# Two block rows of eight products instead of three at the head of the feed-forward input, and another order of the weight sums

## The chip, the cores and the metric

The kernel runs on one core of one Trainium2 chip. The metric is the device time of one execution in microseconds, lower is better. Four compute engines take part: PE (TensorE, the matmuls), DVE (VectorE), ACT (ScalarE) and POOL (GpSimd); SP (SyncE) issues nearly all DMA transfers from one queue, in the order in which they stand there. Each engine works through its own list of instructions in order, and semaphores make one engine wait for another.

## The reference, cut to what matters

One inference step of a two-layer backbone: 512 latent tokens and 128 prompt tokens (T = 640), width 1024, attention in each layer, and behind each attention a gated feed-forward part of inner width 2816. Everything is float32. The part that the change touches is this:

```python
def swiglu(h, w_in, w_out):
    gate, up = jnp.split(h @ w_in, 2, axis=-1)
    return (jax.nn.silu(gate) * up) @ w_out
...
        hp = modulate(rms_norm(xp, norm_ffn[l]), sh2_p, sc2_p)
        hs = modulate(rms_norm(xs, norm_ffn[l]), sh2_s, sc2_s)
        xp = xp + g2_p * swiglu(hp, w_ffn_in[l], w_ffn_out[l])
        xs = xs + g2_s * swiglu(hs, w_ffn_in[l], w_ffn_out[l])
```

## The kernel before, in words

**Layout.** Activations stand feature-major: a tile has 128 features on the partitions and 640 tokens along it, cut in two halves of 320 (HT). The width 1024 is eight such tiles (KT), the inner width 2816 is 22 block rows of 128 (FB).

**Three passes per product.** A float32 operand is split into a high part (a copy in the multiplier's format, made by ACT) and a low part (the rest, by DVE). A product of two operands is then three matmuls: high with high, high with low, low with high (mm3). The first two of the three need only the weight's high part. A matmul of one 128x128 weight tile with one half is 128x320.

**Block row of eight.** For one block row fb, `whole` computes gate and up over both halves: 2 outputs x 2 halves x 8 feature tiles x 3 passes = 96 matmuls. Its two weight tiles (wgu, 128x1024 each, gate and up) are loaded, split by ACT (L173) and DVE (L174), and used as they are. The eight products of the name are gate and up, two halves of tokens, two halves of the width.

**Block row of seven.** All other block rows use a scheme of Strassen's kind on the 2x2 blocks (gate/up by width halves, and token halves by width halves): 7 products of 4 feature tiles x 3 passes = 84 matmuls. It needs sums of the weights and sums of the activations. `seven` makes the weight sums of a row from the two raw tiles ru (up) and rg (gate): wX is ru itself, wW the second half of rg; s13 (L1208, L1209) and s24 (L1212, L1213) are 128x1024 sums built in halves of 512, and wY and wZ are their splits. `split` does the splitting (ACT L1400, DVE L1401). The activation sums D, N, C, E are made once per layer by `add_up` (L316 to L327) from float32 copies of the modulated activations. The seven products go into three PSUM banks, fg, fd and fu, in the order of `ffn`'s second loop: wX with the first block (fg), wY with D (fd), the E product of the row before (`close`), wZ with N (fg), wX with the third block (fu), wZ with the fourth (fd), wY with C (fg). Copies and sums between them (p, u, up, g) are ACT's and DVE's.

**What sets the order.** The code issues work row by row, and the framework's scheduler, at build time, moves each engine's instructions by their dependences and its own costs; so the order on an engine isn't the order of the code. Loads into `rawp` share three buffers of 128x1024, loads into the pool fp under the tag "wr" two buffers in layer 0 and one in layer 1, and a load waits until the last reader of its buffer is done. In layer 0 the two "wr" buffers also hold float32 copies of the activations until `add_up` has read them. The split tiles alternate between two pools (`turn`).

**Around the head of the stage.** Behind attention comes a norm whose two halves end in a matmul with ones (oanp in layer 0, ocnp in layer 1), a logarithm and exponential on ACT (L221, L222), and `ModS.make` (L296 to L314): DVE's multiplication by the norm (h01t or h11t), ACT's or DVE's scale and shift (h32), a high part and a low part (h01q, h11q). In layer 1 the output stage also works with seven products, and `hidden_pair` makes its operands on the fly: for a pair of block rows the tiles op..a, D, N, b, c, C, E, each with an ACT copy, a DVE low part (L1428) and, for most pairs, a store to DRAM (sp..).

Of the kernel before, what the change touches and what calls it, by code (L numbers as in the profile page):

```python
# [11 lines left out]
F32 = mybir.dt.float32  # L12
F32R = mybir.dt.float32r
AF = mybir.ActivationFunctionType
ALU = mybir.AluOpType
# [3 lines left out]
P = 128  # L19
# [32 lines left out]
def body(ctx, tc, xT, vecs, crow, wm0, wm0g1, wm0g, wm1, wA, wNV, wNA, wMK, wMV, wOA, wGQ, wGK, wGV, wOC,  # L52
# [3 lines left out]
    V, S, G = nc.vector, nc.scalar, nc.gpsimd  # L56
# [32 lines left out]
    def bank(name, kind="m"):  # L89
        if kind == "m":  # L90
            return psp.tile([P, 512], F32, tag="m", bufs=4, name=name)
        return ypool["pool"].tile([P, 512], F32, tag=kind, bufs=ypool["tags"][kind], name=name)
# [13 lines left out]
    def f(ap):  # L106
        return ap.bitcast(F32)
# [60 lines left out]
    def unit(src, n, name, lo="v", pool=None, bufs=3):  # L168

        raw = load(src, n, name + "r")  # L170
        t = (pool or wp).tile([P, 2, 1024], F32R, tag="w", bufs=bufs, name=name)
        hi, lw = t[:, 0, :n], t[:, 1, :n]
        S.activation(hi, raw, AF.Copy)  # L173
        (V if lo == "v" else G).tensor_tensor(lw, raw, f(hi), ALU.subtract)  # L174
        return hi, lw
# [350 lines left out]
    with tc.tile_pool(name="start", bufs=1) as big:  # L526
# [14 lines left out]
        m = [mod0(j, lambda j=j: bank(f"mod{j}", "m"), lambda j, half: [raws[j, half][:, q, :] for q in range(2)]) for j in range(4)]  # L541
# [607 lines left out]
                box["m"].make(c, nrm.rs, k)  # L1149
        return box, nxt  # L1150

    FEW = 3, 3
    STAY = 3
    FIRST, SECOND = FO_ORDER[:9], FO_ORDER[9:]

# [42 lines left out]
    def seven(ru, rg, name, fp, split):  # L1198

        n = ru.shape[-1]  # L1200
        m = n // 2
        wX = split(ru, f"wX{name}")
        t = fp.tile([P, 2, 512], F32R, tag="w4", bufs=2, name=f"wW{name}")
        wW = t[:, 0, :m], t[:, 1, :m]
        S.activation(wW[0], rg[:, m:], AF.Copy)
        V.tensor_tensor(wW[1], rg[:, m:], f(wW[0]), ALU.subtract)
        s13 = fp.tile([P, 1024], F32, tag="ws", bufs=2, name=f"s13{name}")[:, :n]
        V.tensor_tensor(s13[:, :m], rg[:, :m], rg[:, m:], ALU.add)  # L1208
        V.tensor_tensor(s13[:, m:], ru[:, :m], rg[:, :m], ALU.add)  # L1209
        wY = split(s13, f"wY{name}")  # L1210
        s24 = fp.tile([P, 1024], F32, tag="ws", bufs=2, name=f"s24{name}")[:, :n]
        V.tensor_tensor(s24[:, :m], s13[:, m:], rg[:, m:], ALU.add)  # L1212
        V.tensor_tensor(s24[:, m:], s24[:, :m], ru[:, m:], ALU.add)  # L1213
        wZ = split(s24, f"wZ{name}")
        return wX, wW, wY, wZ

    def ffn_out_seven(x, nxt, opened, ops, spilt, split, close, last):
# [30 lines left out]
        class Block:  # L1248


            def __init__(self, i, n, c0):
                self.pairs, self.n, self.name = PASSES[i], n, f"o{i}_{n}"
                self.end = i == len(PASSES) - 1
                self.m = m = P * len(self.pairs)
                ru, rg = raw(n, c0, 2 * m, f"ru{self.name}"), raw(n + 4, c0, 2 * m, f"rg{self.name}")
                self.wX, self.wW, self.wY, self.wZ = seven(ru, rg, self.name, fp, split)
                self.held = {}
# [132 lines left out]
    def ffn(l, x, pend, hm, nxt, side, opened):  # L1390
# [80 lines left out]
        step = None  # L1471
        few = FEW[l]
        for fb in range(few):
# [245 lines left out]
    ws = [unit(wGK[v], 1024, f"wgk{v}") for v in range(2)]  # L1719
# [373 lines left out]
```

## Time and profile before

| | |
|---|---|
| median of 3 runs | 1477.95 us (1476.01 to 1478.81) |
| profiled execution, span | 1475.7 us, 2.25 us under the median |
| PE busy | 1440.4 us, 98% |
| DVE busy | 1235.6 us, 84% |
| ACT busy | 783.4 us, 53% |
| POOL busy | 176.0 us, 12% |
| DMA | 231.49 MB, mean 157 GB/s |
| mean granted TensorE clock | 0.996 |
| input stage of layer 0 | from about 370 to 656 us |
| input stage of layer 1 | from about 1051 us |

A row of a timeline has the start in us from the span's start, the duration, engine, line of the kernel, operation, output <- inputs with buffer numbers left out, shape and count; in brackets the idle time just before it and what ended that. Successive rows of one engine overlap a little, since an instruction begins before the one ahead has drained; the distance of two starts, the pitch, is what one instruction costs the engine. A row of a windows table has the stretch, its length, the busy time and count of PE, the weight loads, DVE, ACT and POOL, the granted clock as a share of full speed, and what DMA moved.

### The profile page before, as it was taken

The numbers are of one execution on the slowest core, as the hardware profiler recorded it, in microseconds if no ns is written. First come the engines' busy times: TensorE is split into PE (matmuls) and PEld (weight loads), VectorE is DVE, ScalarE is ACT, GpSimd is POOL, SyncE is SP. The second block draws the span as 40 slices with busy tenths as digits, with TensorE's granted clock in tenths as the row PEclk, the third lists the DMA queues.
The fourth block names the chain that finished last, engine by engine and source line by source line (L and its number), as shares of the span: only waits on it lengthen the run. The fifth ranks groups of instructions, "written<-read, shape, count | busy, mean of one in ns | idle before, by whom it ended". The sixth has DMA issues, their size and how long they took to land.

```text
span 1475.7 us, 25826 instructions
## 1 busy us (share of the span) xinstructions
PE 1440.4 (98%) x9764; PEld 1390.5 (94%) x9764; DVE 1235.6 (84%) x2391; ACT 783.4 (53%) x1539; POOL 176.0 (12%) x270
## 2 busy tenths in 40 slices
PE   5999999999999999999999999999999999999997
PEld 3989978889999999999999999989999999999997
DVE  5877788877998889965997878888899898989976
ACT  5446677853755545531223656672656555555443
POOL 0046635420000000000000122220000000000000
PEclk9999999999999999999999999999999999999999
DMA  9643431025164555568764300115245555548572
GB/s 374 217 153 125 144 115 44 15 90 182 48 214 164 169 167 173 183 232 315 240 224 143 100 30 30 43 39 190 86 167 181 182 175 184 176 145 297 181 267 72
DMA packets 79637, 231.49 MB, mean 157 GB/s; under 512 B 8856, under 2 KB 13240, under 8 KB 79128
## 3 DMA queue, kind: packets, MB, share of 16 engines
q1 hardware_dynamic: 77152, 225.43, 44.8%
q10 hardware_dynamic: 1944, 3.48, 0.7%
q8 instruction: 76, 1.25, 0.3%
q0 software_dynamic: 416, 0.93, 0.2%
q14 instruction: 49, 0.40, 0.1%
HBM read 193.15 MB, written 36.66 MB: 156 GB/s over the span
## 4 chain that ended last, share of the span: by engine, by line
PE 75%; DVE 11%; DMA 5%; ACT 5%; issue 3%; POOL 1%; DVEq 0%; ACTq 0%; SPq 0%; POOLq 0%
PE fg L64 14%; PE fd L64 6%; PE fgo L64 5%; PE fo L64 5%; PE gq L64 4%; PE fu L64 3%; PE fdo L64 2%; PE gs L64 2%; PE go L64 2%; PE nq L64 2%; PE nk L64 1%; PE fuo L64 1%; DVE junk L1660 1%; PE gt L68 1%; DMA wm<-in_wm 1%
## 5 line engine op out<-in xcount | busy, mean ns | idle before, releaser
L1660 DVE SCALAR_TENSOR_TENSOR junk<-wm,cb 128x1024 bf16<-128x1024 f32 x88 | 107.3, 1220 | 6.7 <-DMA wm<-in_wm 5.5
L64 PE MATMUL gq<-h10h,wgq 128*128 128x320 f32 x256 | 66.3, 318 | 0.0
L267 POOL TENSOR_SCALAR h10h<-h10t,gs,mods 128x320 fp32r<-128x320 f32 x4 | 4.0, 992 | 430.8 <-DVE h10t L261 428.5
L1400 ACT ACTIVATE wY<-s 128x1024 fp32r<-128x1024 f32 x38 | 40.3, 1061 | 25.7 <-PE fg L64 21.1
L1928 POOL TENSOR_TENSOR xr<-xw,fn1rs 128x320 f32<-128x320 f32 x2 | 1.7, 858 | 412.9 <-ACT fn1rs L235 412.9
L1400 ACT ACTIVATE wZ<-s 128x1024 fp32r<-128x1024 f32 x38 | 40.1, 1055 | 15.4 <-PE fd L64 10.3
L1401 DVE TENSOR_TENSOR wZ<-s,wZ 128x1024 fp32r<-128x1024 f32 x38 | 46.3, 1220 | 1.4
L1401 DVE TENSOR_TENSOR wY<-s,wY 128x1024 fp32r<-128x1024 f32 x38 | 46.3, 1219 | 0.3
L64 PEld LDWEIGHTS gq<-h10h,wgq 128*128 128x128 f32 x256 | 45.3, 190 | 0.6
L1509 DVE TENSOR_TENSOR sg<-up,sg 128x640 f32<-128x640 f32 x38 | 31.3, 823 | 15.8 <-ACT sg L1508 14.8
L1508 ACT ACTIVATE sg<-fg 128x320 f32<-128x320 f32 x38 | 16.7, 439 | 48.4 <-PE fg L64 48.4
L64 PE MATMUL gq<-h10l,wgq 128*128 128x320 f32 x128 | 39.8, 311 | 0.0
L1530 ACT ACTIVATE p<-fd 128x320 f32<-128x320 f32 x38 | 16.6, 438 | 42.5 <-PE fd L64 42.5
L1865 ACT ACTIVATE gp<-gs,gb,rq 128x640 f32<-128x640 f32 (+1 forms) x40 | 31.8, 796 | 13.4 <-DVE gb L1864 12.0
L64 PE MATMUL fg<-h01E,wW 128*128 128x320 f32 x228 | 36.6, 309 | 1.1 <-DVE g L1540 1.1
L64 PE MATMUL fg<-h01N,wZ 128*128 128x320 f32 x228 | 36.6, 309 | 0.3 <-ACT p L1528 0.3
L64 PE MATMUL fg<-h01C,wY 128*128 128x320 f32 x228 | 36.6, 309 | 0.2 <-ACT u L1534 0.2
L64 PE MATMUL fg<-h11N,wZ 128*128 128x320 f32 x228 | 36.7, 309 | 0.0
L64 PE MATMUL fg<-h01q,wX 128*128 128x320 f32 x228 | 36.7, 309 | 0.0
L64 PE MATMUL fu<-h11q,wX 128*128 128x320 f32 x228 | 36.6, 309 | 0.0
L64 PE MATMUL fd<-h11q,wZ 128*128 128x320 f32 x228 | 36.6, 309 | 0.0
L64 PE MATMUL fd<-h01q,wZ 128*128 128x320 f32 x228 | 36.5, 309 | 0.0
(3421 smaller groups left out, 5313.5 us busy)
## 6 DMA issues: line engine op xcount, KB each, us to landing
wm<-in_wm SPq DMA_DIRECT2D x48, 512.0 KB, 4.3
mraw<-in_wm SPq DMA_DIRECT2D x8, 1024.0 KB, 13.2
mraw<-in_wm SPq DMA_DIRECT2D x14, 512.0 KB, 3.7
wmv<-in_wm0g SPq DMA_DIRECT2D x8, 512.0 KB, 4.0
wm<-in_wm0g SPq DMA_DIRECT2D x8, 512.0 KB, 5.4
ruo<-in_wFO SPq DMA_DIRECT2D x8, 512.0 KB, 4.1
rgo<-in_wFO SPq DMA_DIRECT2D x8, 512.0 KB, 5.5
x<-in_xT SPq DMA_DIRECT2D x8, 320.0 KB, 5.2
```

The source lines that it names most:

```text
L64: cls.last = nc.tensor.matmul(*a, **k)
L68: cls.last = nc.tensor.transpose(*a, **k)
L267: G.tensor_scalar(h[:, c0:c1], t, self.gsl[:, k, 0:1], self.ml[:, self.sh + k, 0:1], ALU.mult, ALU.add)
L1400: S.activation(h, src, AF.Copy)
L1401: V.tensor_tensor(w_, src, f(h), ALU.subtract)
L1508: last = S.activation(sg[:, 0:HT], g[:, :HT], AF.Silu, scale=-1.0)
L1509: V.tensor_tensor(sg, up, sg, ALU.mult)
L1530: S.activation(p5, b5[:, :HT], AF.Copy)
L1660: V.scalar_tensor_tensor(junk, raw, 1.0, cb[:, c, :], ALU.mult, ALU.mult, accum_out=mods[l][:, j0 + i, c:c + 1])
L1865: gexp[h, j] = S.activation(dst, src, AF.Exp, bias=nb, scale=rq[:, j:j + 1], accum_out=ll[:, j:j + 1])
L1928: G.tensor_tensor(x[k][:, c0:c1], root[1][k], nrm.rs[:, c0:c1], ALU.mult)
```

## The change

FEW goes from 3, 3 to 2, 2: block row 2 of each layer leaves the first loop of `ffn` and enters the second, with seven products. In `seven` the statements stand in another order: both halves of s13 come straight behind wX (the half with ru first), then the first half of s24, then wY's split, then s24's second half, then wW, then wZ. The sums and their results are the same; the function serves all rows of seven, and the output stage of layer 1.

```diff
@@ -1149,7 +1149,7 @@
-    FEW = 3, 3
+    FEW = 2, 2
     STAY = 3
@@ -1200,17 +1200,17 @@
         n = ru.shape[-1]
         m = n // 2
         wX = split(ru, f"wX{name}")
+        s13 = fp.tile([P, 1024], F32, tag="ws", bufs=2, name=f"s13{name}")[:, :n]
+        V.tensor_tensor(s13[:, m:], ru[:, :m], rg[:, :m], ALU.add)
+        V.tensor_tensor(s13[:, :m], rg[:, :m], rg[:, m:], ALU.add)
+        s24 = fp.tile([P, 1024], F32, tag="ws", bufs=2, name=f"s24{name}")[:, :n]
+        V.tensor_tensor(s24[:, :m], s13[:, m:], rg[:, m:], ALU.add)
+        wY = split(s13, f"wY{name}")
+        V.tensor_tensor(s24[:, m:], s24[:, :m], ru[:, m:], ALU.add)
         t = fp.tile([P, 2, 512], F32R, tag="w4", bufs=2, name=f"wW{name}")
         wW = t[:, 0, :m], t[:, 1, :m]
         S.activation(wW[0], rg[:, m:], AF.Copy)
         V.tensor_tensor(wW[1], rg[:, m:], f(wW[0]), ALU.subtract)
-        s13 = fp.tile([P, 1024], F32, tag="ws", bufs=2, name=f"s13{name}")[:, :n]
-        V.tensor_tensor(s13[:, :m], rg[:, :m], rg[:, m:], ALU.add)
-        V.tensor_tensor(s13[:, m:], ru[:, :m], rg[:, :m], ALU.add)
-        wY = split(s13, f"wY{name}")
-        s24 = fp.tile([P, 1024], F32, tag="ws", bufs=2, name=f"s24{name}")[:, :n]
-        V.tensor_tensor(s24[:, :m], s13[:, m:], rg[:, m:], ALU.add)
-        V.tensor_tensor(s24[:, m:], s24[:, :m], ru[:, m:], ALU.add)
         wZ = split(s24, f"wZ{name}")
```

Within `seven` the line numbers move: s13 is L1204 and L1205, s24 L1207 and L1209, wW L1212 (ACT) and L1213 (DVE). In the whole program PE has 24 rows of matmul fewer by count, DVE 16 rows more, ACT 11 more; the number of DMAs is the same. A condition in the second loop, `if fb == few or l and fb % 2`, now makes block row 2 the one whose gate tile comes through rawp; in layer 1 row 3 still does too, in layer 0 row 3's gate tile now comes through the "wr" buffers.

DVE in layer 1, ahead of and in block row 2. Before, the place where the low part of the gate and up tiles of row 2 (wgu_20, wgu_21) and of wX_3 stand:

```order
L1445 SCALAR_TENSOR_TENSOR n_1_12965<-sg_1_12960,sg_0_12818 128x320
L1449 TENSOR_TENSOR c_1_12966<-sg_1_12960,sg_0_12818 128x320
L174 TENSOR_TENSOR wgu_21_13006<-wgu_21r,wgu_21_13006 128x1024
L1428 TENSOR_TENSOR op0N<-n_1_12965,op0N 128x320
L1428 TENSOR_TENSOR op0b<-sg_1_12960,op0b 128x320
L1428 TENSOR_TENSOR op0c<-sg_1_12960,op0c 128x320
L1428 TENSOR_TENSOR op0C<-c_1_12966,op0C 128x320
L1451 SCALAR_TENSOR_TENSOR n_1_12965<-n_1_12965,sg_1_12960 128x320
L1401 TENSOR_TENSOR wX_3_13125<-wu_3r,wX_3_13125 128x1024
L1428 TENSOR_TENSOR op0E<-n_1_12965,op0E 128x320
```

and now:

```order
L1428 TENSOR_TENSOR op0C<-c_1_12975,op0C 128x320
L1451 SCALAR_TENSOR_TENSOR n_1_12974<-n_1_12974,sg_1_12969 128x320
L1207 TENSOR_TENSOR s_2_13014<-s_2_13011,wg_2r 128x512
L1401 TENSOR_TENSOR wY_2_13016<-s_2_13011,wY_2_13016 128x1024
L1428 TENSOR_TENSOR op0E<-n_1_12974,op0E 128x320
L1209 TENSOR_TENSOR s_2_13014<-s_2_13014,wu_2r 128x512
L1213 TENSOR_TENSOR wW_2_13020<-wg_2r,wW_2_13020 128x512
L1536 TENSOR_TENSOR up_2_13029<-fu_2_13028,p_2_13031 128x320
L1401 TENSOR_TENSOR wX_3_13118<-wu_3r,wX_3_13118 128x1024
L1401 TENSOR_TENSOR wZ_2_13023<-s_2_13014,wZ_2_13023 128x1024
L1204 TENSOR_TENSOR s_3_13121<-wu_3r,wg_3r 128x512
```

The low parts wgu_20 and wgu_21 are gone from here; wY_2 stands behind op0C and the n of op0E, and wX_3 and wZ_2 behind wY_2. The two halves of s13 stand a few rows higher.

PE in layer 1 at the same place, from the end of block row 2's first two products, now:

```order
L64 MATMUL fu_2_13028<-h11q_12505,wX_2_13008 128x320 x3
L64 MATMUL fd_2_13027<-h11D_12514,wY_2_13016 128x320 x2
L64 MATMUL fg_3_13136<-h11q_12498,wX_3_13118 128x320 x2
L64 MATMUL fu_3_13138<-h11q_12502,wX_3_13118 128x320 x2
L64 MATMUL fd_2_13027<-h11D_12514,wY_2_13016 128x320
L64 MATMUL fd_2_13027<-h11D_12515,wY_2_13016 128x320 x3
L64 MATMUL fd_2_13027<-h11D_12516,wY_2_13016 128x320 x3
L64 MATMUL fd_2_13027<-h11D_12517,wY_2_13016 128x320 x3
L64 MATMUL fg_2_13026<-h11N_12522,wZ_2_13023 128x320 x2
L64 MATMUL fd_2_13027<-h11q_12510,wZ_2_13023 128x320 x2
L64 MATMUL fg_3_13136<-h11q_12498,wX_3_13118 128x320
L64 MATMUL fg_3_13136<-h11q_12499,wX_3_13118 128x320 x3
```

Block row 2 now begins with 12 matmuls of fg and 12 of fu, all on wX_2; then two on wY_2's high part and four on wX_3's; the row that reads fd_2 with h11D once is the first that needs wY_2's low part. Layer 0 has the same order there.

ACT in layer 1, behind the norm's exponential (L222), now:

```order
L221 ACTIVATE ocnrs<-ocnp_12483,eps 128x320
L222 ACTIVATE ocnrs<-ocnrs 128x320
L1400 ACTIVATE wX_2_13008<-wu_2r 128x1024
L305 ACTIVATE h1132l_12488<-h11t_12530,mods_99,gs_103 128x320
L305 ACTIVATE h1132l_12489<-h11t_12544,mods_99,gs_103 128x320
```

Before, the rows of L305 followed L222 directly; now the high part of wX_2 stands between them. On SP, the load of wg_3r stood between the stores of op0D and op0N; now it stands behind the store of op0E.

## The prediction

> **What bounds the kernel now.** I read the page's head first, then busy time by window, then the waits of PE and the timelines around block row 2 of both layers.
>
> ```profile
> span 1475.7 us, 25826 instructions
> PE 1440.4 (98%) x9764; PEld 1390.5 (94%) x9764; DVE 1235.6 (84%) x2391; ACT 783.4 (53%) x1539; POOL 176.0 (12%) x270
> ...
> 1100.00:1200.00 100.00, 100.00 (x684) 100.00 (x683) 93.58 (x147) 59.15 (x102) 0.00 (x0) 1.00 0.53 176
> 400.00:500.00 100.00, 99.74 (x680) 99.39 (x679) 91.11 (x138) 51.76 (x83) 0.00 (x0) 1.00 0.54 185
> ```
>
> A windows row gives the stretch, its length, then busy time (and count) of PE, the weight loads, DVE, ACT and POOL, then the granted clock. TensorE is the bound: inside the feed-forward stages it is busy 99.7 to 100% at clock 1.00. One 128x320 matmul thus takes 100/684 = 0.1462 us, a product of 12 takes 1.754 us. DVE is no distant second there: 91 to 94%. So what decides is whether DVE has each low part ready in time at the two places where the work is regrouped. Elsewhere PE never waits, so time lost there is not won back later.
>
> **What is removed.** A block row of eight takes 96 matmuls, one of seven 84; one row per layer changes: 24 x 0.1462 = 3.51 us, 1.754 per layer. That is the gain if nothing waits.
>
> **What DVE gets.** Pitches (start to start, back to back) from the two stages:
>
> ```profile
> 405.35 1.21 DVE L174 TENSOR_TENSOR wgu<-wgu_20r,wgu 128x1024 fp32r<-128x1024 f32 x1
> 406.49 0.48 DVE L327 TENSOR_TENSOR h01D<-h0132a,h01D 128x320 fp32r<-128x320 f32 x1
> 406.89 0.48 DVE L327 TENSOR_TENSOR h01N<-h01n,h01N 128x320 fp32r<-128x320 f32 x1
> ...
> 409.63 0.82 DVE L1461 TENSOR_TENSOR hd_0l<-sg,hd_0h 128x640 fp32r<-128x640 f32 x1
> 410.37 1.22 DVE L1401 TENSOR_TENSOR wX<-wu_3r,wX 128x1024 fp32r<-128x1024 f32 x1
> ...
> 1090.98 0.69 DVE L1208 TENSOR_TENSOR s<-wg_3r 128x512 f32<-128x512 f32 x1
> 1091.58 0.69 DVE L1209 TENSOR_TENSOR s<-wu_3r,wg_3r 128x512 f32<-128x512 f32 x1
> ```
>
> A 128x1024 low part is 1.14 us, 128x320 is 0.40, 128x640 is 0.74, 128x512 is 0.60. On DVE a row of eight costs two low parts, two 128x320 and one 128x640: 2.28 + 0.80 + 0.74 = 3.8 us under 14.04 us of PE. A row of seven costs wX, wY, wZ (3.42), four half sums and wW (3.00), two ups and g2 (1.20), the 128x640 product and one more 128x640 pass (1.48): 9.1 us under 12.28 us. So DVE gets 5.3 us more in a stretch where it is nearly full, and most is due before the row's second product.
>
> **Layer 0.** wX_2 is made early, while DVE waits for the second norm:
>
> ```profile
> L165 SPq DMA_DIRECT2D wgu_20r<-in_wFI x2: 328/328/328, 359.9 to 1041.2; - x2
> DMA to landing us min/median/max: 4.5/4.5/4.5
> ...
> 367.93 0.70 PE L64 MATMUL oanp<-oansql,ones 128*128 128x320 f32 x2
> ...
> 369.73 1.30 DVE L298 TENSOR_TENSOR h01t<-xr,oanrs 128x320 f32<-128x320 f32 x3 [4.23 <-ACT oanrs L222]
> ```
>
> The load that takes wgu_20r's place lands at 359.9 + 4.5 = 364.4; high part and low part (at most 1.14 each) end near 366.7, the residual and its square behind them (two 128x320 passes, 0.48 each) near 367.7, PE asks at 367.93. The idle 4.23 us hides it with 0.2 us to spare; without that cover it costs up to 1.14. I take 0.2.
>
> ```profile
> 381.46:411.50 30.04, 30.04 (x204) 29.74 (x204) 29.35 (x64) 23.24 (x48) 0.00 (x0) 1.00 0.31 108
> 405.93 0.75 PE L64 MATMUL fg<-h01q,wgu 128*128 128x320 f32 x4
> 431.09 0.60 PE L64 MATMUL fg<-h01q,wX 128*128 128x320 f32 x3
> ```
>
> DVE works without a break from 381.46 to the end of hd_0l, 410.37. In the new order the same stretch loses the low parts of wgu_20 and wgu_21 (-2.28) and takes two halves of s13 (+1.20), the first of s24 (+0.60) and wY_2 (+1.14): wY_2's low part ends at 411.03. Then come s24's second half, wW, up, wX_3, wZ_2: 0.60 + 0.60 + 0.40 + 1.14 + 1.14 = 3.88, so wZ_2's low part ends at 414.91. PE starts block row 2 at 405.93 and has only 30 matmuls that need neither (4.39 us, to 410.3); it waits 0.7 for wY_2, then does 22 (3.22 us) and waits 0.66 for wZ_2. From there 104 matmuls (15.21 us) lead to the end of row 3's C product: 430.12, against 431.09 before. So layer 0 keeps 0.97 of its 1.75; less 0.2 for the head, **-0.8 us**. Bounds: -1.75 (DVE not late), +0.5 (the head misses by 1.14 and one more half sum is late).
>
> At the end of layer 0's input stage PE waits once:
>
> ```profile
> 654.19 1.22 DVE L1660 SCALAR_TENSOR_TENSOR junk<-wm,cb 128x1024 bf16<-128x1024 f32 x1
> ...
> 655.88 0.41 PE L64 MATMUL fg<-h01E,wW 128*128 128x320 f32 x1 [1.14 <-DVE g L1540]
> ```
>
> The modulation passes (junk) of three wm tiles stand ahead of that g; in the new order those of only one do, with two 128x768 low parts instead. I take **-0.75** of the 1.14; bounds -1.14 and +0.5, since the two low parts are as long as the pass they replace.
>
> **Layer 1.** Here the same step has a longer DVE queue ahead of it, because five operand sums of the output stage (op0N, b, c, C and the two sums) stand before wY_2.
>
> ```profile
> 1056.24:1089.34 33.10, 33.10 (x226) 32.73 (x224) 32.39 (x73) 25.88 (x56) 0.00 (x0) 1.00 0.27 85
> 1080.71 1.33 PE L64 MATMUL fg<-h11q,wgu 128*128 128x320 f32 x8
> 1088.94 0.48 DVE L1428 TENSOR_TENSOR op0E<-n,op0E 128x320 fp32r<-128x320 f32 x1
> 1105.53 0.75 PE L64 MATMUL fg<-h11q,wX 128*128 128x320 f32 x4
> ```
>
> DVE runs from 1056.24 (second half of the norm) to the end of op0E, 1089.34, with 0.7 us of gaps. The new stretch up to wY_2's low part loses two wgu low parts (2.28), wX_3 (1.14) and op0E (0.40), and gains s13 (1.20), s24's half (0.60) and wY_2 (1.14): -0.88, so it ends at T = 1088.46. Then op0E, s24's other half, wW, up, wX_3, wZ_2: 0.40 + 0.60 + 0.60 + 0.40 + 1.14 + 1.14 = 4.28, wZ_2's low part at 1092.74. PE starts row 2 at 1080.71 and is out of work after 30 matmuls, at 1085.10: it stands **3.4 us** for wY_2, then, after 22 more, 1.1 us for wZ_2. The 104 matmuls from there end at 1107.95, against 1105.53: **+2.4 us**, the 1.75 us saved already inside.
>
> Two things come on top. wX_2 is queued on ACT between the norm's exponential and the first modulated tiles, and must wait for its load (1041.2 + 4.5 = 1045.7):
>
> ```profile
> 1045.08 2.29 ACT L305 ACTIVATE h1132l<-h11t,mods,gs 128x320 f32<-128x320 f32 x4 [0.56 <-DVE h11t L298]
> ...
> 1044.56:1056.24 11.68, 11.68 (x78) 11.36 (x77) 10.92 (x28) 7.04 (x13) 1.96 (x4) 1.00 0.02 8
> ```
>
> Its high part ends near 1046.7, so these start 1.6 us later; behind them wait DVE's casts and the second half's statistics. DVE has 0.76 us free up to 1056.24 and gets 1.14 more: at least 0.4 late; also PE's norm matmul now stands two matmuls (0.29 us) later. I take **+0.5**, bounds 0.3 and 1.6. And wg_3r now comes through the same three buffers as wu_2r, wg_2r and wu_3r: its load waits for s24's second half (T + 1.0 + 0.5 = 1090.0), where before it was asked for at 1081.04 and found its buffer free:
>
> ```profile
> 1081.04 0.33 SPq L165 DMA_DIRECT2D wg_3r<-in_wFI  x1
> ...
> 1089.45 0.76 SPq L1431 DMA_DIRECT2D sp0E<-op0E  x1
> ...
> DMA to landing us min/median/max: 3.5/4.5/5.4
> ```
>
> On SP it is also moved past the five stores sp0N to sp0E. It lands at about 1094.5 (3.5 to 5.4 after 1090.0), DVE wants it at 1093.2 for s13 of row 3, and ACT's queue (wW_3, then u_2, which PE's C product needs) stands on it too. wY_3's low part follows 3.54 us after it (1.20 + 0.60 + 0.60 + 1.14), at 1098.0; PE asks for it 34 matmuls plus two past 1093.2, at 1098.5, and for C at 1096.2 against u_2 near 1095.6. So at 4.5 it just fits, at 5.4 it costs 0.4, and with the stores' traffic beside it up to 1.5. I take **+0.5**.
>
> All other rows of seven, in both stages, get the new order but the same work; PE did not wait there. I take 0, bounds -0.5 and +0.5.
>
> **Sum.** -0.8 - 0.75 + 2.4 + 0.5 + 0.5 = +1.85 us on the 1475.7 us span: 1477.6. The span lies 2.25 us under the median of the runs (1477.95) and that stays, so **1479.8 us**. Its own range is 1477.5 to 1482.0.
>
> **Rivals.** 0.2% (3 us) is about what a measurement can tell from no change: faster is below 1475.0, slower above 1480.9.
>
> *All hidden.* If the DVE order ahead of wY_2 moves up where it has gaps, or PE reaches row 2 later than I think, the whole 3.51 stays, and with the 0.75: 1473.7. Against it: DVE at 32.39 of 33.10 us in layer 1 leaves no 4 us. For it: only my reading of the queue puts wY_2 so late. 0.12.
>
> *The clock falls in layer 1's gap.* This trace has such a case:
>
> ```profile
> 202.37 0.50 PE L64 MATMUL no<-nts_0l,nv 128*128 128x512 f32 x1 [1.67 <-DVE nts_0l L402]
> ...
> 204.34 0.46 PE L64 MATMUL mk<-ckph,wm 128*128 128x256 f32 x1 [0.85 <-DVE nm L784]
> ...
> 207.48 0.47 PE L64 MATMUL mq<-cqs0h,wm 128*128 128x320 f32 x1
> 207.74 0.39 PE L64 MATMUL mq<-cqs1h,wm 128*128 128x320 f32 x1
> 204.00:208.00 4.00, 3.66 (x17) 3.67 (x18) 3.44 (x14) 2.85 (x11) 1.19 (x3) 0.57 0.00 0
> ```
>
> After gaps of 1.67 and 0.85 us the granted clock is 0.57 for 4 us, and a 128x320 matmul takes 0.26 us instead of 0.146. The new gap is 3.4 us. Half speed for 3.4 us costs 1.7 us; 1.1 of it may lie under the wait for wZ_2, so +0.6 to +1.7 more, and with wg_3r late by its 1.5 the sum passes +3 and decides for slower: 1482.0. The single stall of 1.14 us at 654.74 is too short to tell. 0.22.
>
> [...]
>
> *Layer 0 loses too.* wX_2's load lands late by 1 us in the head, or the new order makes each row's wW or wZ late by a little (0.1 us in 38 rows is 3.8): 1483. Against: DVE has 6 to 11% free in steady rows. 0.10.
>
> **How the numbers follow.** Forecast 0.56, all hidden 0.12, clock 0.22, layer 0 and rows 0.10. Faster: 0.10 of the all-hidden case. Slower: 0.13 of the forecast's own spread, 0.17 of the clock's, 0.09 of the last: 0.39. Same: 0.51. The range 1476.0 to 1483.3 leaves out the all-hidden case and the far end of the last.
>
> **What would show it.** A PE wait on wY or wX_3 of about 3 to 4 us, once, near 1085 in layer 1, and under 1.5 near 410 in layer 0; PE's count 24 lower; ACT's wX_2 ahead of h1132l; wg_3r issued near 1090; no wait on g at the end of layer 0. I am wrong if layer 1 has no wait over 1 us at row 2, or if waits appear in the steady rows, or if the granted clock falls behind row 2.

## The result, and the profile after

The changed kernel takes 1481.59 us (median of 5 runs, 1479.38 to 1482.33), the kernel before 1476.01 us beside it (5 runs, 1475.22 to 1478.81): ratio 1.0036, 95% interval 1.0025 to 1.0046. It is slower, by 3.7 to 6.8 us. The prediction said 1479.8 us, likeliest no change that can be told, with a chance of 0.39 for slower: the direction of its sum is right, its size is too small (+1.85 us, where the medians differ by 5.6). The profiled execution's span is 1479.6 us, 3.9 us over the one before.

The page of the changed kernel, span and busy time:

```profile
span 1479.6 us, 25798 instructions
PE 1440.9 (97%) x9740; PEld 1387.1 (94%) x9740; DVE 1245.0 (84%) x2407; ACT 791.7 (54%) x1549; POOL 174.7 (12%) x270
```

PE has the 24 matmuls less that were named, which should be 3.5 us, yet its busy time is up by 0.5 us: some matmuls took longer, ten of them shown below. DVE has 9.4 us more. PE's timeline at block row 2 of layer 1:

```profile
1081.16 1.92 PE L64 MATMUL fg<-h11q,wX 128*128 128x320 f32 x12
1086.81 0.56 PE L64 MATMUL fd<-h11D,wY 128*128 128x320 f32 x2 [1.97 <-ACT wY L1400]
1087.76 0.56 PE L64 MATMUL fg<-h11q,wX 128*128 128x320 f32 x2 [0.38 <-ACT wX L1400]
1089.03 3.03 PE L64 MATMUL fd<-h11D,wY 128*128 128x320 f32 x10 [0.41 <-DVE wY L1401]
1094.16 1.63 PE L64 MATMUL fg<-h11N,wZ 128*128 128x320 f32 x10
1109.41 1.92 PE L64 MATMUL fg<-h11q,wX 128*128 128x320 f32 x12
```

The gap ahead of wY_2 is there, in three pieces of 1.97, 0.38 and 0.41 us, because the products between need only high parts. The ten matmuls at 1089.03 take 2.83 us to the next product; at 0.146 us each they would take 1.46. The windows around it (stretch, length, busy time and count of PE, weight loads, DVE, ACT, POOL, then the granted clock) say why:

```profile
1084.00:1086.00 2.00, 0.84 (x6) 0.57 (x4) 2.00 (x6) 1.74 (x5) 0.00 (x0) 1.00 0.00 0
1086.00:1088.00 2.00, 0.80 (x3) 0.54 (x4) 2.00 (x6) 2.00 (x3) 0.00 (x0) 1.00 0.78 296
1088.00:1090.00 2.00, 1.59 (x8) 1.32 (x8) 2.00 (x4) 0.07 (x1) 0.00 (x0) 0.72 0.95 357
1090.00:1092.00 2.00, 2.00 (x9) 2.00 (x9) 2.00 (x3) 1.06 (x1) 0.00 (x0) 0.50 0.86 264
```

DVE is busy 2.00 of every 2 us while PE has 0.8; behind the gap the clock falls to 0.50. DVE's timeline at the same place:

```profile
1087.76 1.22 DVE L1401 TENSOR_TENSOR wY<-s,wY 128x1024 fp32r<-128x1024 f32 x1
1092.03 1.22 DVE L1401 TENSOR_TENSOR wZ<-s,wZ 128x1024 fp32r<-128x1024 f32 x1
1093.87 0.69 DVE L1204 TENSOR_TENSOR s<-wu_3r,wg_3r 128x512 f32<-128x512 f32 x1 [0.61 <-DMA wg_3r<-in_wFI]
```

wZ_2's low part ends at 1093.17, 12.0 us behind the row's first product at 1081.16. The sum had 1092.74 against 1080.71, also 12.0. DVE's queue was read to within 0.1 us; what was added behind it was not.

The head of that stage, from the timelines of ACT, of DVE and of the weight loads (PE waits with its weight load there):

```profile
1044.92 1.06 ACT L1400 ACTIVATE wX<-wu_2r 128x1024 fp32r<-128x1024 f32 x1 [1.34 <-DMA wu_2r<-in_wFI]
```

```profile
1043.61 2.10 DVE L298 TENSOR_TENSOR h11t<-xr,ocnrs 128x320 f32<-128x320 f32 x5 [2.53 <-ACT ocnrs L222]
1046.02 1.23 DVE L1401 TENSOR_TENSOR wX<-wu_2r,wX 128x1024 fp32r<-128x1024 f32 x1 [0.30 <-ACT wX L1400]
...
1056.71 0.89 DVE L298 TENSOR_TENSOR h11t<-xr,ocnrs 128x320 f32<-128x320 f32 x2
```

```profile
1054.02 0.30 PEld L64 LDWEIGHTS ocnp<-ocnacc,ones 128*128 128x128 f32 x2 [0.93 <-DVE ocnacc L212]
1060.63 0.30 PEld L64 LDWEIGHTS fg<-h11q,wgu 128*128 128x128 f32 x2 [0.37 <-DVE h11q L308]
1065.21 0.74 PEld L64 LDWEIGHTS fg<-h11q,wgu 128*128 128x128 f32 x5 [0.32 <-DVE wgu L174]
```

The only such wait of the kernel before:

```profile
1063.83 0.19 PEld L64 LDWEIGHTS fg<-h11q,wgu 128*128 128x128 f32 x1 [0.19 <-ACT h11q L307]
```

PE waits three times on DVE between the stage's start (1050.27; before 1051.22) and row 2. Row 2 comes 30.89 us after the start instead of 29.49. DVE begins the norm's first half 6.66 us ahead of the stage in both traces (before at 1044.56), but comes to the second half 13.10 us later instead of 11.68: the low part of wX_2 (1.14 us) and the wait of 0.30 us for its high part lie between.

Layer 0, row 2 and the last product of its input stage, PE's timeline:

```profile
411.58 0.56 PE L64 MATMUL fg<-h01q,wX 128*128 128x320 f32 x2 [0.39 <-ACT wX L1400]
...
655.26 1.00 PE L64 MATMUL fg<-h01E,wW 128*128 128x320 f32 x5 [0.86 <-DVE g L1540]
```

The wait for g was 1.14 us before. And one wait that no step of the prediction names. In layer 0's output stage, PE and DVE of the changed kernel:

```profile
704.96 0.41 PE L64 MATMUL fo_6a<-hd_1h,wo 128*128 128x320 f32 x1 [0.92 <-DVE wo L1577]
```

```profile
701.74 0.55 DVE L333 SCALAR_TENSOR_TENSOR xr<-fo,mods,xr 128x320 f32<-128x320 f32 x1 [1.80 <-PE fo L64]
...
704.09 0.81 DVE L1577 TENSOR_TENSOR wo<-wo_60r,wo 128x640 fp32r<-128x640 f32 x1
```

ACT of the changed kernel, which makes what the low part needs,

```profile
698.81 0.74 ACT L1576 ACTIVATE wo<-wo_60r 128x640 fp32r<-128x640 f32 x1 [7.51 <-DMA wo_60r<-in_wFO]
```

and DVE of the kernel before:

```profile
699.73 0.82 DVE L1577 TENSOR_TENSOR wo<-wo_60r,wo 128x640 fp32r<-128x640 f32 x1 [0.20 <-ACT wo L1576]
```

The low part of wo_60 used to stand ahead of the residual xr; now it stands behind it, and DVE idles 1.80 us for that residual's product while the low part's input has been ready since about 699.5. The scheduler ordered a stage anew that the diff doesn't touch.

The two spans differ by less than the medians, and the traces show why. In attention the profiled execution of the kernel before had half the clock for 3.41 us:

```profile
868.00:870.00 2.00, 2.00 (x10) 1.96 (x9) 0.66 (x3) 0.91 (x3) 0.00 (x0) 0.50 0.00 0
```

and that of the changed kernel didn't:

```profile
868.00:870.00 2.00, 2.00 (x17) 1.98 (x16) 1.83 (x5) 1.83 (x4) 0.15 (x1) 1.00 0.00 0
```

The work there is the same in both. Of the 14 traces of this study (these two and twelve experiments) four show the fall at this place (the kernel before, and the experiments "filled", "pair later" and "all deferred" below), ten don't, with no relation to what was changed (the last section has the columns counted there). It is worth about 1.6 us (half of 3.41 us is the most that it can be); so the changed kernel's true loss is nearer 3.9 + 1.6 = 5.5 us, which is what the medians show (5.6).

### The profile page after: what moved, and what is told of

Same layout as the page of the kernel before. It is cut to its first block, busy times and chain, and to the rows that moved or that the text cites. A ratio compares the mean times of both kernels' runs of the same rounds, so it can differ in the third digit from the quotient of the medians.

```text
span 1479.6 us, 25798 instructions
## 1 busy us (share of the span) xinstructions
PE 1440.9 (97%) x9740; PEld 1387.1 (94%) x9740; DVE 1245.0 (84%) x2407; ACT 791.7 (54%) x1549; POOL 174.7 (12%) x270
## 3 DMA queue, kind: packets, MB, share of 16 engines
q8 instruction: 76, 1.25, 0.4%
## 5 line engine op out<-in xcount | busy, mean ns | idle before, releaser
L64 PE MATMUL fd<-h11D,wY 128*128 128x320 f32 x240 | 40.0, 316 | 2.4 <-ACT wY L1400 2.0
L64 PEld LDWEIGHTS fd<-h11D,wY 128*128 128x128 f32 x240 | 37.1, 193 | 2.9 <-ACT wY L1400 2.2
L64 PE MATMUL fg<-h11q,wX 128*128 128x320 f32 x240 | 39.0, 309 | 0.4 <-ACT wX L1400 0.4
```

What stands on the lines that cost most here:

```text
L64: cls.last = nc.tensor.matmul(*a, **k)
```

## The experiments

All are timed in five rounds beside the kernel before, and the ratio goes by that; its median was 1476.09 us beside the first four kernels of the table that follow the change, 1476.63 beside the next four, 1475.75 beside the next three and 1475.52 beside the last. Two offsets from PE's timelines serve as the yardstick for layer 1: from the stage's first product to row 2's first product, and to row 4's first product (the end of row 3's C product). The last column is the longest wait of PE on an operand of rows 2 and 3 there.

| kernel | median us | ratio to before, 95% | to row 2 | to row 4 | longest wait |
|---|---|---|---|---|---|
| before | 1476.01 | | 29.49 | 54.31 | none |
| the change | 1481.59 | 1.0036 [1.0025, 1.0046] | 30.89 | 59.14 | 1.97 on wY_2 |
| layer 0 only | 1476.4 | 1.0001 [0.9992, 1.0010] | | 54.22 | none |
| layer 1 only | 1480.34 | 1.0029 [1.0020, 1.0038] | 30.87 | 59.78 | 1.95 on wY_2 |
| new order only | 1475.19 | 0.9996 [0.9988, 1.0005] | | 54.24 | none |
| old order, rows moved | 1484.05 | 1.0057 [1.0044, 1.0070] | 31.10 | 60.57 | 4.15 on wY_2 |
| gap filled | 1481.77 | 1.0032 [1.0020, 1.0045] | 31.05 | 58.58 | 0.39 on wY_2 |
| wX_2 late | 1481.79 | 1.0031 [1.0019, 1.0042] | 29.64 | 58.66 | 2.35 on wX_2 |
| pair later | 1477.35 | 1.0003 [0.9994, 1.0011] | 30.64 | 55.15 | 0.72 on wY_2 |
| low parts on POOL | 1483.38 | 1.0049 [1.0035, 1.0063] | 30.98 | 61.83 | 4.03 on wY_2 |
| early operands | 1480.72 | 1.0032 [1.0022, 1.0042] | 31.13 | 56.53 | 1.76 on wZ_2 |
| early, pair later | 1476.33 | 1.0005 [0.9996, 1.0014] | 31.13 | 53.99 | none |
| all deferred | 1476.54 | 1.0003 [0.9994, 1.0011] | 31.27 | 54.23 | none |
| head cleared | 1480.16 | 1.0028 [1.0018, 1.0038] | 30.27 | 56.46 | 1.20 on p, row 3 |

**Which part of the change costs.** Three kernels undo one part each; the first keeps the change in layer 0 alone, the second in layer 1 alone, the third has the new order with no row moved.

The edit of the first is this; the second has 3, 2 in its place and the third 3, 3.

```diff
-    FEW = 2, 2
+    FEW = 2, 3
```

> Block row 2 is one of seven in layer 0 only (2, 3), with the new order of the weight sums. Theory A (the loss is layer 1's late wY_2 and wZ_2 and the clock that falls in the gap; layer 0 gains a little): 0.5 to 1.5 us faster than before, ratio 0.999 to 0.9997, no PE wait over 1.2 us in the input stages. Rival R1 (the new order costs a little in every row): 2 us slower or more. Rival R2 (both layers lose alike): about 2 us slower.

> Block row 2 is one of seven in layer 1 only (3, 2), with the new order. Theory A: 4 to 6 us slower than before, ratio 1.003 to 1.004, with the same PE waits at row 2 (about 2.0, 0.4 and 0.4 us) and granted clock 0.5 to 0.7 for 3 to 4 us behind them. R1: 2 to 4 us slower but with small waits spread over the rows. R2: about 2 us slower.

> Three rows of eight as before, only the new order of the weight sums. Theory A: within 0.7 us of before (ratio 0.9995 to 1.0003), no PE wait over 0.5 us in the rows of seven. R1: 2 to 4 us slower. R2: same as before.

Layer 1 alone carries most of the loss (+4.3 us). The order alone costs nothing and may gain a little. In the traces its gain is plain: from the second norm matmul of layer 0 (367.93 in the kernel before) to row 4's first product, PE takes 63.16 us before, 62.61 with the order only, 62.65 with layer 0 only and 62.64 with the change; from there to the output stage 222.16 before and 221.64 in each of these three. So the 0.5 us won around row 2 of layer 0 is the order's doing. The seven products, which take 1.75 us from PE there, add nothing to it: DVE already sets that stretch (in the trace of the change it has no gap there from 399.8 to 420 us). And the late low part of wo_60 (0.92 us of wait, 1.2 us on the way) is in all kernels with row 2 of layer 0 moved and in none of the others. Layer 0 alone being 0.7 us behind the order alone (1.0001 against 0.9996) fits that, but the intervals don't tell the two apart.

**What the order is worth once the rows are moved.** The rows are moved, but `seven` keeps the statements of the kernel before.

```diff
+        t = fp.tile([P, 2, 512], F32R, tag="w4", bufs=2, name=f"wW{name}")
+        wW = t[:, 0, :m], t[:, 1, :m]
+        S.activation(wW[0], rg[:, m:], AF.Copy)
+        V.tensor_tensor(wW[1], rg[:, m:], f(wW[0]), ALU.subtract)
         s13 = fp.tile([P, 1024], F32, tag="ws", bufs=2, name=f"s13{name}")[:, :n]
-        V.tensor_tensor(s13[:, m:], ru[:, :m], rg[:, :m], ALU.add)
         V.tensor_tensor(s13[:, :m], rg[:, :m], rg[:, m:], ALU.add)
+        V.tensor_tensor(s13[:, m:], ru[:, :m], rg[:, :m], ALU.add)
+        wY = split(s13, f"wY{name}")
...
```

> Two rows of eight, with the old order of the weight sums. In layer 1 wY_2's low part then stands 1.4 us of DVE work later, wZ_2's at the same place. Theory A: as slow as the change or up to 1 us slower (3.5 to 6.5 us over before), since wZ_2 sets when row 2 can go on; the gap before wY_2 about 1 us longer. R1: faster than the change by 2 us or more, close to before. R2: as the change.

It is 2.5 us slower than the change, more than was expected. The waits of PE in both layers, and the clock:

```profile
413.50 0.56 PE L64 MATMUL fd<-h01D,wY 128*128 128x320 f32 x2 [1.42 <-ACT wY L1400]
414.44 0.67 PE L64 MATMUL fg<-h01q,wX 128*128 128x320 f32 x2 [0.39 <-ACT wX L1400]
...
1092.86 0.56 PE L64 MATMUL fd<-h11D,wY 128*128 128x320 f32 x2 [4.15 <-ACT wY L1400]
```

```profile
416.00:418.00 2.00, 2.00 (x9) 2.00 (x9) 2.00 (x3) 0.78 (x1) 0.00 (x0) 0.50 0.99 299
```

The old order has the second half of s13 late, so even wY_2's high part is late, and the gap isn't broken by products on high parts. The new order is what keeps the move from costing 8 us.

**What the clock costs.** Twenty matmuls without use are put into the gap of layer 1, so that PE doesn't idle.

```diff
+            if l and fb == few:
+                for _ in range(20):
+                    PE.matmul(b5[:, :HT], wX[0][:, 0:P], hm.operand(11)[0][0], start=True, stop=True)
```

> The change, with 20 extra matmuls of 128x320 in layer 1 between block row 2's first and second product, on tiles that are there already (their sums are overwritten; nothing else changes). They take 2.9 us of a gap of about 3.5 us in which PE does nothing. Theory C (the clock that falls in the gap costs about 0.9 us): granted clock stays at 1.00 behind the gap, ten matmuls of fd take 1.46 us instead of 2.8, 0.5 to 1 us faster than the change (about 1480.5). Rival (the wait for wZ_2's low part is the bound whatever the clock): same as the change. Second rival (the extra matmuls push the work behind them): 1 to 2 us slower than the change.

PE's timeline, then the window in which the change had 0.50:

```profile
1088.85 1.73 PE L64 MATMUL fd<-h11D,wY 128*128 128x320 f32 x10 [0.39 <-DVE wY L1401]
```

```profile
1090.00:1092.00 2.00, 1.48 (x9) 0.92 (x8) 2.00 (x4) 1.22 (x2) 0.00 (x0) 1.00 0.88 286
```

The clock stays at 1.00, and row 4 comes 0.56 us sooner than in the change; most of what the faster matmuls win goes into the wait for wZ_2. The clock is a real term, some 0.6 us in the trace, and not the cause. The medians don't show it (1481.77 against 1481.59).

**Is it only the place of wX_2?** Layer 1's wX_2 is split behind the modulation of the norm's second half.

```diff
-            wX, wW, wY, wZ = seven(ru, rg, f"{l}_{fb}", fp, split)
+            first = [l and fb == few]
...
+            def late(src, name):
+                if first.pop() if first else False:
+                    return after(hm.act[7, 1], lambda: split(src, name))
+                return split(src, name)
...
+            wX, wW, wY, wZ = seven(ru, rg, f"{l}_{fb}", fp, late)
```

> The change, with layer 1's wX_2 made behind the second half of the modulation (its high part on ACT behind the last modulated tile) instead of in the norm's head. Theory H (the head is late because ACT waits there for wX_2's load and DVE makes its low part, 1.4 us in all): the PE wait on the norm (0.7 us) is gone, but DVE has the same 1.14 us to do later, so wZ_2's low part ends within 0.4 us of where it did; PE's gap is cut in two and the clock falls less: 0 to 1.3 us faster than the change. Rival (the head is what makes the row late): 1.4 us faster or more. Second rival (DVE's total work ahead of wZ_2 is the bound and nothing else): same as the change.

The wait in the head is gone, row 2 comes 1.25 us sooner than in the change, and at once waits for the low part that was moved:

```profile
1083.60 2.48 PE L64 MATMUL fg<-h11q,wX 128*128 128x320 f32 x10 [2.35 <-DVE wX L1401]
```

Row 4 comes at 58.66 against 59.14. Moving one DVE pass from ahead of the row into it moves the wait and keeps the sum: what counts is the total of DVE's work ahead of wZ_2.

**Taking work out of DVE's queue ahead of wY_2.** The operands of the second block row for the output stage (`hidden`, 8 passes of 0.40 us) are deferred behind row 2's weight sums.

```diff
-            hidden(fb, sg)
+            if l and fb in (1,):
+                owed.append((fb, sg))
+            else:
+                hidden(fb, sg)
...
+            while owed:
+                after(lows[-1], lambda: hidden(*owed.pop(0)))
```

> The change, with layer 1's operands of pair 0's second row (two sums, then N, b, c, C, E: eight 128x320 passes on DVE, 3.2 us) moved behind block row 2's weight sums. Theory A (DVE's queue ahead of wY_2 and wZ_2 is the cause): wY_2 and wZ_2 come about 2.8 and 3.6 us earlier, no PE wait over 1 us at row 2, clock 1.00; the moved passes make row 3's wY late by 1 to 2 us instead; 2 to 4 us faster than the change (1477.5 to 1479.5). Rival (something else than DVE's order holds row 2, a load or ACT): within 1 us of the change.

PE's timeline and the window:

```profile
1085.99 0.56 PE L64 MATMUL fd<-h11D,wY 128*128 128x320 f32 x2 [0.72 <-ACT wY L1400]
...
1106.10 1.92 PE L64 MATMUL fg<-h11q,wX 128*128 128x320 f32 x12
```

```profile
1086.00:1088.00 2.00, 1.61 (x9) 1.35 (x10) 2.00 (x4) 1.05 (x2) 0.00 (x0) 1.00 0.40 104
```

With 3.2 us taken out of the queue the kernel is 4.2 us faster than the change and the wait falls to 0.72 us; the clock stays at 1.00 there. That is the theory of the prediction, shown: the move costs what DVE is late.

**Taking it to another engine instead.** Fifteen low parts go to POOL, which is busy 12% of the span.

```diff
-                V.tensor_tensor(t[:, HT:T], src, f(t[:, 0:HT]), ALU.subtract)
+                (G if c in "CE" and self.name == "h11" else V).tensor_tensor(t[:, HT:T], src, f(t[:, 0:HT]), ALU.subtract)
...
-            V.tensor_tensor(t[:, HT:T], src, f(t[:, 0:HT]), ALU.subtract)
+            (G if p == 0 else V).tensor_tensor(t[:, HT:T], src, f(t[:, 0:HT]), ALU.subtract)
```

> The change, with 15 low parts of 128x320 in layer 1 made by POOL instead of DVE (the C and E sums of the activations and all seven operands of pair 0): DVE is relieved of 6.0 us ahead of row 2 and row 3, nothing is put off. Theory A: no wait at row 2, layer 1 gives its 1.75 us less the head's 1.4; 4 to 6 us faster than the change, 0.5 to 2 us faster than before (1474 to 1475.5). Rival (POOL, about 0.86 us for each, is late itself or slows DVE): PE waits on fg with E or C, or DVE's passes longer than 0.48; as the change or slower.

It is slower than the change, by 1.8 us in the medians and 2.7 us at row 4; the intervals of the two ratios overlap. Timelines of DVE and of POOL ahead of wY_2, and PE's wait:

```profile
1082.51 1.34 DVE L1204 TENSOR_TENSOR s<-wu_2r,wg_2r 128x512 f32<-128x512 f32 x1
1083.77 1.34 DVE L1205 TENSOR_TENSOR s<-wg_2r 128x512 f32<-128x512 f32 x1
1085.04 0.68 DVE L1207 TENSOR_TENSOR s<-s,wg_2r 128x512 f32<-128x512 f32 x1
```

```profile
1082.20 1.10 POOL L327 TENSOR_TENSOR h11C<-h1132u,h11C 128x320 fp32r<-128x320 f32 x1
1083.26 1.30 POOL L327 TENSOR_TENSOR h11E<-h1132l,h11E 128x320 fp32r<-128x320 f32 x1
```

```profile
1086.26 0.90 PE L64 MATMUL fd<-h11D,wY 128*128 128x320 f32 x2 [4.03 <-ACT wY L1400]
```

The two halves of s13 take DVE 1.34 us each while POOL works, where they take 0.69 in the change, with POOL idle; the next sum of that size takes 0.68, with POOL through. What POOL takes over it takes back from DVE, in these rows.

**Loading and summing early.** In layer 1 the first up tile goes into a buffer that is free long before, so its split precedes the norm, and the weight sums of row 2 are made as soon as the first half of the norm is through. The second kernel also defers the pair, the third the operands of the first block row too, and two low parts of C in each layer.

```diff
+            if l and fb == few:
+                ru = fp.tile([P, 1024], F32, tag="wr", bufs=1, name=f"wu{l}_{fb}r")
+                nc.sync.dma_start(ru, wFI[l, fb, 1])
...
-            wX, wW, wY, wZ = seven(ru, rg, f"{l}_{fb}", fp, split)
+            wX, wW, wY, wZ = seven(ru, rg, f"{l}_{fb}", fp, split, hm.low[7, 0] if l and fb == few else None)
```

> The change, but layer 1's first w_upper quarter is loaded into a buffer that is free long before (so its low pass and ScalarE's product wX_2 are done before the norm's last stretch), and row 2's weight sums are made early on VectorE. Theory (VectorE and ScalarE come to row 2 of layer 1 late because of where the pair's operands stand in their queues): the wait of the first product on wX_2 and the extra 1.4 us ahead of the row go, the late wZ_2 comes some 1 to 2 us sooner, VectorE's 0.6 us wait on the last weight load goes: 2 to 4 us faster than the change, 1477.5 to 1479.5 us, ratio to the kernel before 1.001 to 1.002. Rival (the change's 4 to 5 us in layer 1 come from the clock that falls in the gap, and the loads' places don't matter): a gap of about 2 us ahead of fd on wY stays, the clock falls again, 1481 to 1482 us.

> The same early load and early sums, and the second pair's operands of layer 1 (8 passes of VectorE, about 3.2 us) moved behind row 2's weight sums. Theory: both what made VectorE late and the head's extra wait are taken away; no wait over 0.7 us is left in layer 1's row 2 and 0.5 to 1 us is gained over the kernel with the move alone (1477.35): 1474 to 1476.5 us, 0 to 2 us faster than the kernel before. Rival (the early sums put VectorE late with the other half of the norm's operands, so that what is won behind the row is lost ahead of it): 1477 to 1479 us, with a longer wait at ocnp or h11 ahead of row 2.

> The same, with the pair operands of both rows 2 and 3 deferred and, in both layers, two low parts of the C block placed behind wY_2's low part. Theory (VectorE's queue ahead of wY_2 and wZ_2 sets the end of row 2 in both layers): waits on wY_2 under 0.5 us in both layers, layer 0 keeps its 0.7 to 0.9 us gain, 1473.5 to 1476 us, 0 to 2.5 us faster than the kernel before. Rival (what is deferred is then late itself for row 3): a new wait of 1 to 2 us on hidden operands in row 3 of a layer, 1476 to 1479 us.

The early operands alone miss what was expected of them: the head's 1.4 us doesn't go, and the wait on wY_2 is replaced by one on wZ_2. DVE and PE of that kernel:

```profile
1040.56 1.22 DVE L1400 TENSOR_TENSOR wX<-wu_2r,wX 128x1024 fp32r<-128x1024 f32 x1
1041.70 0.55 DVE L331 SCALAR_TENSOR_TENSOR xr<-oc,mods,xr 128x320 f32<-128x320 f32 x1
...
1056.38 0.69 DVE L1203 TENSOR_TENSOR s<-wu_2r,wg_2r 128x512 f32<-128x512 f32 x1
```

```profile
1090.55 1.74 PE L64 MATMUL fg<-h11N,wZ 128*128 128x320 f32 x10 [1.76 <-DVE wZ L1400]
```

In the head DVE has work of row 2 in the way again. wX_2's low part stands ahead of the residual (xr), so the norm's first multiplication begins 5.78 us ahead of the stage instead of 6.66 (1044.77, with the stage at 1050.55), and a half of s13 stands ahead of the norm's second half. wW_2's high part stands on ACT where wX_2's stood, but holds nothing up: the first modulated tile begins 0.53 us behind that multiplication, 0.52 us in the kernel before.

Its trace is of an execution of 1478.86 us, under the median of 1480.72; what the others lost beyond it no trace shows. With the pair deferred as well no wait is left in rows 2 and 3, and row 4 comes at 53.99: 0.3 us sooner than before, of the 1.75 us that the seven products save. The kernel comes out level with the one before (1.0005), as does the one with everything deferred.

**Clearing the head.** To the last kernel two holds are added: the weight sums of row 2 wait for tile 5 of the norm's second half on DVE, wW_2 for the same tile on ACT.

```diff
-            wX, wW, wY, wZ = seven(ru, rg, f"{l}_{fb}", fp, split, hm.low[7, 0] if l and fb == few else None)
+            wX, wW, wY, wZ = seven(ru, rg, f"{l}_{fb}", fp, split, *((hm.low[5, 1], hm.act[5, 1]) if l and fb == few else ()))
```

> The same as the kernel with all deferrals, but in layer 1 the weight sums of row 2 wait on VectorE until the modulated tile 5 of the second half is split, and ScalarE's wW_2 stands behind that tile's modulation, so neither the norm's head nor the second half has any operand of row 2 in its way. Theory (the rest of the change's loss is the 1.4 to 1.8 us that PE loses between the start of layer 1's stage and row 2, because something of row 2 stands ahead of the modulated tiles on ScalarE or VectorE): row 2 of layer 1 starts 29.5 to 30 us after the stage, instead of 31.2, no wait on wY_2 or wZ_2 over 0.5 us, 1472 to 1475 us, 1 to 3 us faster than the kernel before. Rival (PE waits there on the norm whatever stands in the queues): row 2 still starts 31 us behind the stage, 1475 to 1477 us.

Row 2 comes 0.9 us sooner than in the others (30.27), so part of the head was the queues' doing. So is the 0.8 us that is left against the kernel before: wX_2's low part still stands ahead of the residual (at 1039.39), and the norm's first multiplication begins 5.77 us ahead of the stage (1043.60, with the stage at 1049.37). The rival, that PE waits on the norm whatever stands in the queues, isn't borne out. Row 4 comes 2.2 us later than with everything deferred, because row 3 now waits on what was pushed back:

```profile
1090.18 0.56 PE L64 MATMUL fd<-h11D,wY 128*128 128x320 f32 x2 [1.04 <-ACT wY L1403]
1091.94 2.02 PE L64 MATMUL fg<-h11N,wZ 128*128 128x320 f32 x12 [1.20 <-ACT p L1545]
```

The expected 1 to 3 us over the kernel before didn't come. No kernel tried beats the one before by more than its interval.

## Why the prediction was right, and where it was off

Term by term, on the spans of the two profiled executions:

| step | predicted us | measured us |
|---|---|---|
| head of layer 0 up to row 2 | +0.2 | +0.9, of it 0.7 at the second norm matmul, which stands anywhere from 367.3 to 368.7 in the traces (370.2 in one) |
| layer 0, row 2 to the end of row 3's C | -0.97 | -0.73 |
| steady rows, layer 0 | 0 | -0.5 |
| wait on g | -0.75 | -0.3 |
| layer 0's output stage, wo_60 | not named | +1.2 |
| attention, clock | not named | -1.6, chance |
| head of layer 1 | +0.5 | +1.4 |
| layer 1, DVE late with wY_2 and wZ_2 | +2.4 | +2.4, worked out from the end of wZ_2's low part |
| clock behind the gap | a rival, +0.6 to +1.7 | +0.6 to +1.0 |
| load of wg_3r | +0.5 | 0 |

The rest, 0.1 to 0.5 us, lies in stretches that scatter by as much. Without the chance fall of the clock the sum measured is 5.5 us where 1.85 was forecast. Up to layer 1's stage the forecast was -1.55 and 0.65 us was lost; in layer 1's input stage it was +3.4 and 4.9 came.

**DVE's queue was the mechanism**, in the place and at the size named. The gap, its cause, and that taking 3.2 us out of that queue takes the loss away are shown. The gap's form differed: the prediction had 3.4 us ahead of wY_2's low part; PE waited 1.97 us already for the high part, then did six matmuls on high parts between.

**The head of layer 1 was mis-sized.** The prediction had bounds of 0.3 and 1.6 us and took 0.5; 1.4 us came. It counted DVE's 0.76 us of slack as cover for the low part's 1.14. That slack covered nothing. It is two waits, 0.34 us for ACT and 0.35 for POOL, that come behind the new work in the same chain, and they are still there (0.32 and 0.35). So the whole 1.14 us and the new wait of 0.30 for wX_2's high part, 1.44 together, came through. Idle time covers new work only if the work can run in it.

**The clock's rival came in**, together with the forecast and not in place of it. By the prediction's own list of signs it was wrong on this ("or if the granted clock falls behind row 2"). Behind the gaps of 1.97, 0.38 and 0.41 us it was 0.50 for 3.41 us, though PE had 1.64 us of work in 1084 to 1088. What the clock costs was 0.6 us by the filled gap (58.58 against 59.14), or 1.0 us by what lies between the end of wZ_2's low part (1093.17) and the product that needs it (1094.16).

**wg_3r's load did what was said and cost nothing.** It is issued late, at 1090.01, and DVE waits 0.61 us for it; but with PE itself late by then nothing waits for DVE. A cost was put on top of another that covers it.

**The wait on g** shrank by 0.3, not 0.75 us, so the sign "no wait on g" failed too: the two low parts of wo stand where two of the passes over wm stood. This was the bound that the prediction named on the other side.

**Layer 0's output stage was not looked at.** The prediction compared the engines' order only around the two input stages. The order is made when the program is built, so the same comparison in that stage would have found the low part of wo_60 behind the residual, where the trace has it.

**The range and the median.** 1481.59 lies inside 1476.0 to 1483.3 and 0.7 us above the 1480.9 from which the prediction counted slower. Its base was 1477.95, the median of three runs, and the trace of one that had lost its clock once; with five runs the kernel before stands at 1476.01. Put on that base, the forecast is 1477.9 us and its range ends at 1481.4, just under the measured time. That the time lies inside the range is thus luck: the base stood 1.9 us too high and the sum 3.7 us too low. What was right is the mechanism and the sign.

## What to carry to other kernels

Where one engine is nearly full, a change that takes work from the bound and gives three times as much to the full one must be costed by that engine's queue up to the first operand wanted, not by the bound's count; and what is deferred must be followed to the place where it is wanted in turn. After a change to a scheduled program, compare the order of every stage, the untouched ones too. Compare profiled executions only with their clock beside them: here one fall of 3.41 us hid about 1.6 of 5.5 us.

## What the runs showed of the hardware

**In these traces the clock fell behind stretches of 3.41 us whose matmuls had few columns (at most 3092 of some 7470), and the size of a gap didn't tell.** It fell to 0.50 behind 1.42 and 0.39 us (old order, layer 0), behind 1.97, 0.38 and 0.41 (the change), behind 2.35 (wX_2 late); it fell in attention with no gap over 0.26 us in the rows there, beside ten matmuls of 128x2; it stayed at 1.00 behind 1.76 us (early operands) and behind 1.04 and 1.20 (head cleared). So the size of the gap alone doesn't sort these cases.

Cut where the granted clock changes, the traces show more. From 30 us to the last matmuls each fall lasts 3.41 us, or twice that (layer 1 only, low parts on POOL). The times between falls are whole multiples of one length: in the change 880.64 us from 208.25 to 1088.89, 258 times 3.4133, and in the kernel before 658.77 us from 207.91 to 866.68, 193 times 3.4133. Stretches of the change, of the old order and of the early operands:

```profile
1085.48:1088.89 3.41, 1.42 (x6) 0.89 (x6) 3.41 (x7) 2.59 (x4) 0.00 (x0) 1.00 0.72 273
1088.89:1092.31 3.42, 3.28 (x12) 3.17 (x12) 3.42 (x7) 1.27 (x2) 0.00 (x0) 0.50 0.90 292
...
1090.60:1094.01 3.41, 0.76 (x3) 0.50 (x4) 3.41 (x7) 2.47 (x3) 0.00 (x0) 1.00 1.02 387
1094.01:1097.42 3.41, 3.41 (x14) 3.41 (x14) 3.41 (x5) 1.06 (x1) 0.00 (x0) 0.50 0.97 298
...
1089.28:1092.69 3.41, 2.14 (x14) 2.14 (x15) 3.41 (x6) 0.37 (x1) 0.00 (x0) 1.00 1.01 397
1092.69:1096.11 3.42, 3.42 (x26) 3.42 (x25) 3.40 (x6) 2.26 (x4) 0.00 (x0) 1.00 0.76 302
```

Behind these stretches with 6 and 3 matmuls comes one at half the clock, behind the one with 14 the clock stays. Counted are the columns of the matmuls begun in a stretch: 320 for one of 128x320, 2 for one of 128x2; at 0.1462 us each, 23.3 of 128x320 fill a stretch, some 7470 columns. Over all 14 traces, from 30 to 1460 us, and of the stretches that ran at full clock themselves, each of the 13 with up to 2560 columns was followed by a fall, so were 5 of the 13 with 2708 to 3092, and none of the 5819 with more was. That covers attention's fall: the stretch ahead of it in the kernel before is busy for 2.90 us, but has 2772 columns. The other traces cut the same work elsewhere: the change has 2772 there too, without a fall, the nine others without a fall 3092 to 4692. So the same work went with a fall in four traces and with none in ten. Ahead of 30 us, where matmuls with 128x32 weights run, this count doesn't sort the falls, and no kernel was made to test it.

**POOL and DVE were slower side by side.** With the fifteen low parts on POOL, a 128x512 sum of two inputs took DVE 1.34 us while POOL ran a two-input pass of 1.10 us, and another while it ran one of 1.30; the sum behind them, with POOL through, took 0.68. POOL's 128x320 passes of that kind took 0.86 to 0.89 us in the change, the fifteen moved ones 0.88 to 1.85. Both slow sums ended 0.55 us behind a pass of POOL (1083.85 behind 1083.30, 1085.11 behind 1084.56). What in the two engines makes them slower no run shows.
